# Inverse roots of the attention norms moved from GpSimd's power to ScalarE's logarithm and exponential, page scales made earlier, modulation rows started later

## The chip, the cores and the metric

The kernel runs on one core of a Trainium2 chip. The metric is the device time of one launch in microseconds (us). Beside the timed runs there is one execution recorded by the hardware profiler; its rows give, for every engine, what ran when. The engines are PE (matrix products, with its weight loads as PEld), DVE (vector work), ACT (scalar functions), POOL (GpSimd) and SP, which here issues every DMA.

## The reference, cut to what matters

One transformer layer on a sequence of 1024 rows with 1024 channels, in float32. Two attention groups of eight heads share an input projection: chunked attention over a band (CA, head width 64) and latent attention (MLA, with a low-rank q of 256 and kv of 128, and heads of 64 + 32). All of their norms are root-mean-square norms, and it is the inverse roots of these that the change concerns:

```python
def rmsnorm(x, g):
    xf = x.astype(jnp.float32)
    y = xf * lax.rsqrt(jnp.mean(xf * xf, axis=-1, keepdims=True) + EPS)
    return (y * g.astype(jnp.float32)).astype(x.dtype)
...
    mod = jnp.dot(jax.nn.silu(c), w_ada[l]) + b_ada[l]
    sh_a, sc_a, g_a, sh_m, sc_m, g_m = jnp.split(mod, N_MOD, axis=-1)
    h = modulate(rmsnorm(x, g_attn_norm[l]), sh_a, sc_a)
    proj = jnp.dot(h, w_in[l])
    q_lat, kv_lat, k_rope, ca_qkv = jnp.split(proj, split_pts, axis=-1)
    q = jnp.dot(rmsnorm(q_lat, g_q_latent[l]), w_q_up[l])      # 8 heads x 96
    kv = jnp.dot(rmsnorm(kv_lat, g_kv_latent[l]), w_kv_up[l])  # 8 heads x (64 + 64)
    k = concatenate([k_nope, k_rope of all heads])
    q, k = rmsnorm(q, g_mla_q[l]), rmsnorm(k, g_mla_k[l])      # then rope on the last 32
    ...
    cq, ck = rmsnorm(ca[:, :, 0], g_ca_q[l]), rmsnorm(ca[:, :, 1], g_ca_k[l])
    ...
    x = x + g_a * (concat(o_mla, o_ca) @ w_out)
    h = modulate(rmsnorm(x, g_mlp_norm[l]), sh_m, sc_m)
    x = x + g_m * ((silu(gate) * val) @ w_down)                # conv of width 3 before silu
```

## The kernel before

All products are float32 made of three products of split values: each operand is cut into a `hi` part and a residue `lo` (helpers `hi_of` and `lo_of`, lines 73 to 82; their rows in the profile all say L77 or L82, whichever engine they are given). Instructions are written in program order for a tile scheduler, which fixes each engine's order when the kernel is built: it lets an instruction go ahead of earlier ones by modelled times and priorities, and `tc.issue_after(x)` adds an order by hand. A tile from a pool with n buffers waits until the tile n back is no longer read. At run time every engine works through its own list in order, and so does SP, whose DMAs wait for their buffers.

*The start (to about 70 us).* SP loads constants, the eight x tiles, `c_rep`, the weights `adaw` of the first modulation (`load_ada`, line 207, sixteen tiles in five buffers), and the gains. `page_scales` (line 220) reduces gains and bias table to power-of-two scales, some 36 small DVE instructions, one of them fed by a product over `ones` and one by a POOL power. The loop at line 263 makes the x norms. Then the loop at line 362 runs over eight blocks d of 128 channels: two DVE reductions with `adaw` (L369) give shift and scale of the block, `mod_transpose` (line 341) turns x, applies them on ACT and splits the result into pages hT[d, h] (h = 0: `hi` on ACT and residue on POOL; h = 1: `hi` on POOL and residue on DVE), and PE starts the first q/k projection from each page.

*The attention (to 710 us).* The score and value blocks of 32 units (`Unit`: one head and half of the queries; first 16 of CA, then 16 of MLA) are laid out one after another; between the blocks `pace` takes steps from `fillers`, the generators that make what later units need: `f_v(0)`, `f_qk(1)`, `f_qk(2)`, `f_v(1)`, `f_qk(3)`, `f_m` (the latents), `f_up(0)` and `f_up(1)` (MLA's up-projections, `f_up_steps`, line 581) and `f_oca`. Beside them `f_ada` (line 483) makes twelve pieces of later modulation rows, each from eight loads `aw` of 128 KB and eight DVE products into `aacc` (L492 for the first, L494 for the others). Loads and sums share pool A of three buffers.

*The norms.* `qk_norm` (line 416), the loop in `f_m` (line 539) and that in `f_up_steps` (line 606) follow one scheme. ACT copies the projection out of PSUM and squares it, DVE sums per head (or ACT while squaring, for the latents), and POOL takes the inverse root by `rsqrt_mean`:

```python
    def rsqrt_mean(r, ss, n, cols=None):
        sc = ss if cols is None else ss[:, cols]
        pool.tensor_scalar(sc, sc, 1.0 / n, EPS, op0=MUL, op1=ADD)
        pool.tensor_tensor(r, ss, nhalf[:].to_broadcast(list(r.shape)), op=ALU.pow)
```

Then POOL (CA, latents, MLA's rope part of k) or DVE (MLA's q and the rest of k) multiplies by the root. In `f_up_steps` q and k of a tile have sums and roots of their own (`uss`/`ur` and `kss`/`kr`), and POOL adds the rope part's `ssr` to k's (L641). The `raw` copies come from four buffers (`rtile`), the squares from two (`qtile`).

*Value tiles.* `v_tile` (line 448) takes a tile from a rotating pool and lets POOL set its columns of ones and zeros: for CA from six buffers at each use, for MLA eight tiles. POOL also sets the rows of ones of the key pages `kts` and the row buffer `mz` (L694 to L696).

After 710 us follow the output projection, the second norm (`r2`, one column at a time, by `rsqrt_mean`) and the channel layer, in which PE is busy nearly all the time.

Of the kernel before, what the change touches and what calls it, by code (L numbers as in the profile page):

```python
# [23 lines left out]
P = 128  # L24
# [38 lines left out]
def layer_kernel(ctx, tc, I, out):  # L63
# [3 lines left out]
    def f32(ap):  # L67
        return ap.bitcast(F32)
# [12 lines left out]
    def lo_of(eng, o, i, hi):  # L81
        (pool if eng == "p" else dve).tensor_tensor(o, i, f32(hi), op=SUB)  # L82
# [40 lines left out]


# [72 lines left out]

    xs = []
# [142 lines left out]
    def mod_transpose(src, k, h, row, pspool, psum_tag, pb, hpool, tag, tmp, nbuf, heng, leng):  # L341

        pt = pspool.tile([P, 512], F32, name=f"ht_ps{row}_{k}_{h}", tag=psum_tag, bufs=pb)
        for j in range(4):
            pe.transpose(pt[:, j * P:(j + 1) * P], src(j), ident[:])
        pg = hpool.tile([P, 2, 512], F32R, name=f"hT{row}_{k}_{h}", tag=tag, bufs=nbuf)
        a, b = modT[:, row, k:k + 1], modT[:, row + 1, k:k + 1]
        v = tmp.tile([P, 512], F32, name=f"hv{row}_{k}_{h}", tag="hv", bufs=2)
        if heng == "a":
            act.activation(pg[:, 0], pt[:], AF.Identity, scale=a, bias=b)  # L350
        act.activation(v[:], pt[:], AF.Identity, scale=a, bias=b)
        if heng != "a":
            hi_of(heng, pg[:, 0], v[:])
        lo_of(leng, pg[:, 1], v[:], pg[:, 0])
        return pg

    hT = {}
# [58 lines left out]
    def qk_norm(src_psum, nm, qn, j0):  # L416
# [8 lines left out]
        rsqrt_mean(r[:], ss[:], HD)  # L425
# [22 lines left out]
    def v_tile(pl, name, tag, bufs):  # L448
        v = pl.tile([P, 4, 2, 3, 64], F16, name=name, tag=tag, bufs=bufs)
        pool.memset(v[:, :, 0, 1], 1.0)  # L450
        pool.memset(v[:, :, 1, 1], 0.0)
        return v
# [30 lines left out]
    def f_ada():  # L483
        for m in (2, 3, 4):
            for n in range(4):
                acc = atile(f"aacc{m}_{n}")
                c0 = m * D + n * 256
                for k in range(ND):
                    w = atile(f"aw{m}_{n}_{k}")
                    sp.dma_start(w[:], I["w_ada"][k * P:(k + 1) * P, c0:c0 + 256])  # L490
                    if k == 0:
                        dve.tensor_scalar(acc[:], w[:], cs[:, 0:1], None, op0=MUL)  # L492
                    else:
                        dve.scalar_tensor_tensor(acc[:], w[:], cs[:, k:k + 1], acc[:], op0=MUL, op1=ADD)  # L494
                    if k % 2 and k < ND - 1:
                        yield 0
# [39 lines left out]
    def f_m():  # L536
        w = load_w("wm_", I["w_m"], NM)
        lat = {}
        for t in range(NT):
# [12 lines left out]
            pool.tensor_scalar(ss[:, 0:1], ss[:, 0:1], 1.0 / QR, EPS, op0=MUL, op1=ADD)  # L552
            rsqrt_mean(r[:], ss[:], KVR, cols=slice(1, 2))
# [27 lines left out]
    def f_up_steps(gr):  # L581
        if gr == 0:
            right.__exit__(None, None, None)
            for i in "4v3":
                G["cm" + i] = tc.tile_pool(name="gp" + i, bufs=1, side="right", reuse_waits="tile")
                G[i] = G["cm" + i].__enter__()
        wq = []
# [18 lines left out]
        for t in range(NT):  # L606
            h, j = divmod(t, 4)
            sl = slice(j * P, (j + 1) * P)
            if t % 2 == 0:
                mq[gr, t // 2] = g3([P, 2, 4, QK], F32, f"qn{gr}_{t}")  # L610
                mk[gr, t // 2] = g3([P, 2, 4, QK], F32, f"kn{gr}_{t}")
                mv[gr, t // 2] = v_tile(G["v"], f"vt{gr}_{t}", "Gv", 8)
# [3 lines left out]
            raw = rtile(f"uqr{gr}_{t}")  # L616
            act.activation(raw[:, :384], pt[:, :384], AF.Copy)
            sq = qtile(f"usq{gr}_{t}")
            act.activation(sq[:, :384], raw[:, :384], AF.Square)
            ss = cst.tile([P, 4], F32, name=f"uss{gr}_{t}", tag="ss", bufs=4)  # L620
            r = cst.tile([P, 4], F32, name=f"ur{gr}_{t}", tag="rr", bufs=4)
            dve.tensor_reduce(ss[:], sq[:, :384].rearrange("p (a b) -> p a b", a=4), axis=AX.X, op=ADD)
            rsqrt_mean(r[:], ss[:], QK)
            q_t = mq[gr, t // 2][:, t % 2]
            dve.tensor_tensor(q_t, raw[:, :384].rearrange("p (a b) -> p a b", a=4),
                              r[:].unsqueeze(2).to_broadcast([P, 4, QK]), op=MUL)
            rope_apply(q_t[:, :, NOPE:], q_t[:, :, NOPE:], tabq, t, 4, raw[:, 0:256])
# [10 lines left out]
            ss = cst.tile([P, 4], F32, name=f"kss{gr}_{t}", tag="ss", bufs=4)  # L638
            r = cst.tile([P, 4], F32, name=f"kr{gr}_{t}", tag="rr", bufs=4)
            dve.tensor_reduce(ss[:], s3, axis=AX.X, op=ADD)  # L640
            pool.tensor_tensor(ss[:], ss[:], ssr[:, t:t + 1].to_broadcast([P, 4]), op=ADD)  # L641
            rsqrt_mean(r[:], ss[:], QK)
            k_t = mk[gr, t // 2][:, t % 2]
            dve.tensor_tensor(k_t[:, :, 0:NOPE], r3, r[:].unsqueeze(2).to_broadcast([P, 4, NOPE]), op=MUL)
            pool.tensor_tensor(k_t[:, :, NOPE:], kr[:, t:t + 1, :].to_broadcast([P, 4, ROPE]),
                               r[:].unsqueeze(2).to_broadcast([P, 4, ROPE]), op=MUL)
# [47 lines left out]
    for x in kts:  # L694
        pool.memset(x[64:65, 1], 1.0)
    pool.memset(mz[:], 0.0)  # L696
# [585 lines left out]
```

## Time and profile before

| | |
|---|---|
| timed runs | 1506.06, 1506.7, 1516.16 us; median 1506.7 |
| profiled execution | 1507.0 us, of which its span 1505.2 |
| mean granted PE clock | 0.945 |
| PE busy | 1323.0 us (88%), 6926 products |
| DVE busy | 1011.6 us (67%) |
| POOL busy | 818.5 us (54%) |
| ACT busy | 715.4 us (48%) |
| DMA | 153.02 MB, mean 102 GB/s |

Times are microseconds from the start of the span. An engine's busy time is a mean over stages of different kinds, so the prediction reads it stage by stage. In a group's row stand line, engine, operation, tiles out<-in with their sizes, the count, then busy time and mean ns, and behind the last bar the time in which the engine stood idle just before, with the instruction that ended most of it. In a row of the timeline the first number is the start and the second the length.

### The profile page before, as it was taken

The numbers are of one execution on the slowest core, as the hardware profiler recorded it, in microseconds if no ns is written. First come the engines' busy times: TensorE is split into PE (matmuls) and PEld (weight loads), VectorE is DVE, ScalarE is ACT, GpSimd is POOL, SyncE is SP. The second block draws the span as 40 slices with busy tenths as digits, with TensorE's granted clock in tenths as the row PEclk, the third lists the DMA queues.
The fourth block names the chain that finished last, engine by engine and source line by source line (L and its number), as shares of the span: only waits on it lengthen the run. The fifth ranks groups of instructions, "written<-read, shape, count | busy, mean of one in ns | idle before, by whom it ended". The sixth has DMA issues, their size and how long they took to land.

```text
span 1505.2 us, 19968 instructions
## 1 busy us (share of the span) xinstructions
PE 1323.0 (88%) x6926; PEld 1054.2 (70%) x6926; DVE 1011.6 (67%) x1421; ACT 715.4 (48%) x1319; POOL 818.5 (54%) x901
## 2 busy tenths in 40 slices
PE   3769999898868899988928759999999999999997
PEld 2769879776745556655716648888888887887885
DVE  8926665555667866565676668777777888666563
ACT  5435565454756766665453324444444433333331
POOL 5764444353698443322867245555556554665662
PEclk9979999999977999999958979999999999999999
DMA  8421223221110023324521142222222234446442
GB/s 308 124 67 50 64 61 111 80 74 43 57 35 8 18 82 98 103 81 149 211 98 56 56 154 84 85 84 84 78 77 84 85 123 172 147 145 231 163 140 98
DMA packets 80001, 153.02 MB, mean 102 GB/s; under 512 B 8214, under 2 KB 44314, under 8 KB 79900
## 3 DMA queue, kind: packets, MB, share of 16 engines
q1 hardware_dynamic: 79900, 151.75, 30.5%
q8 instruction: 54, 0.88, 0.3%
q14 instruction: 47, 0.39, 0.1%
HBM read 122.88 MB, written 28.84 MB: 101 GB/s over the span
## 4 chain that ended last, share of the span: by engine, by line
PE 34%; DVE 18%; POOL 16%; DMA 16%; issue 10%; ACT 5%; DVEq 0%; SPq 0%; POOLq 0%; ACTq 0%
DMA aw<-w_ada 7%; POOL wds L82 4%; DMA wu<-w_up 4%; PE tm L815 3%; DVE u L1132 3%; PE dnp L1196 2%; PE dnp L1197 2%; PE dnp L1198 2%; PE p L1126 2%; PE p L1124 2%; PE p L1125 2%; DVE aacc L494 2%; DVE wu L1154 2%; DVE u L1133 2%; DVE adaw L369 1%
## 5 line engine op out<-in xcount | busy, mean ns | idle before, releaser
L82 POOL TENSOR_TENSOR wds<-wd,wds 128x512 fp32r<-128x512 f32 x88 | 152.9, 1756 | 100.2 <-ACT wds L75 100.2
L75 ACT ACTIVATE wds<-wd 128x512 fp32r<-128x512 f32 x88 | 54.6, 624 | 152.2 <-PE dnp L1198 149.6
L1196 PE MATMUL dnp<-wds,g 128*128 128x512 f32 x308 | 119.7, 390 | 2.3 <-DVE c L1158 1.5
L1186 DVE TENSOR_TENSOR wd<-wd,gmbc 128x1024 f32<-128x1024 f32 x44 | 69.9, 1588 | 76.3 <-DMA wd<-w_down 76.2
L1198 PE MATMUL dnp<-wds,g 128*128 128x512 f32 x308 | 118.5, 390 | 2.2 <-DVE g L82 2.2
L1197 PE MATMUL dnp<-wds,g 128*128 128x512 f32 x308 | 119.7, 389 | 0.0
L82 POOL TENSOR_TENSOR wc<-ws,wc 128x512 fp32r<-128x512 f32 x22 | 55.4, 2520 | 74.2 <-ACT wc L75 74.2
L494 DVE SCALAR_TENSOR_TENSOR aacc<-aw,cs,aacc 128x256 f32<-128x256 f32 x84 | 45.4, 541 | 62.5 <-DMA aw<-w_ada 62.1
L82 POOL TENSOR_TENSOR wa<-wu,wa 128x512 fp32r<-128x512 f32 x22 | 36.7, 1669 | 90.6 <-ACT wa L75 90.6
L815 PE MATMUL tm<-qt,kt 96*128 96x512 f16 (+7 forms) x288 | 74.1, 346 | 7.7 <-ACT qt L778 4.7
L826 DVE TENSOR_TENSOR hlm<-pm,hlm 128x512 f16<-128x512 f32 (+1 forms) x96 | 58.3, 615 | 32.6 <-POOL hlm L77 17.8
L1132 DVE SCALAR_TENSOR_TENSOR u<-c,pk,u 128x1023 f32<-128x1023 f32 x44 | 75.5, 1724 | 4.1 <-ACT u L1131 4.1
L82 DVE TENSOR_TENSOR g<-gr,g 128x512 fp32r<-128x512 f32 x44 | 70.6, 1607 | 9.9 <-ACT g L75 9.9
L819 ACT ACTIVATE pc<-tc,sca 128x512 f32<-128x512 f32 (+3 forms) x96 | 50.2, 524 | 47.5 <-DVE hlc L826 27.9
L815 PEld LDWEIGHTS <-kt 128*128 128x128 f16 (+2 forms) x480 | 47.4, 102 | 35.2 <-issue 16.8
L77 POOL TENSOR_SCALAR hlm<-pm 128x384 f16<-128x384 f32 (+2 forms) x48 | 24.8, 516 | 82.9 <-ACT pm L819 65.1
L1196 PEld LDWEIGHTS dnp<-wds,g 128*128 128x128 f32 x308 | 57.8, 188 | 15.6 <-ACT wds L75 1.9
L1198 PEld LDWEIGHTS dnp<-wds,g 128*128 128x128 f32 x308 | 57.8, 188 | 15.0 <-DVE g L82 3.0
L819 ACT ACTIVATE pm<-tm,scm 128x512 f32<-128x512 f32 (+1 forms) x96 | 55.3, 579 | 27.2 <-PE tm L815 20.6
L1131 ACT ACTIVATE u<-c,pk 128x1024 f32<-128x1024 f32 x44 | 52.3, 1236 | 32.9 <-DVE c L1164 32.9
L826 DVE TENSOR_TENSOR hlc<-pc,hlc 128x512 f16<-128x512 f32 (+3 forms) x96 | 52.8, 553 | 22.5 <-POOL hlc L77 11.9
L1197 PEld LDWEIGHTS dnp<-wds,g 128*128 128x128 f32 x308 | 57.8, 188 | 11.9
(432 smaller groups left out, 4703.1 us busy)
## 6 DMA issues: line engine op xcount, KB each, us to landing
wu<-w_up SPq DMA_DIRECT2D x44, 512.0 KB, 3.5
wd<-w_down SPq DMA_DIRECT2D x44, 512.0 KB, 3.6
aw<-w_ada SPq DMA_DIRECT2D x96, 128.0 KB, 2.1
g_d<-u SPq DMA_DIRECT2D x22, 512.0 KB, 2.6
gr<-g_d SPq DMA_DIRECT2D x44, 256.0 KB, 2.8
x<-x SPq DMA_DIRECT2D x16, 512.0 KB, 7.1
adaw<-w_ada_a SPq DMA_DIRECT2D x16, 512.0 KB, 5.1
wq_r<-w_qk SPq DMA_DIRECT2D x32, 128.0 KB, 2.4
```

Of the source, the lines that this page charges most:

```text
L75: act.activation(o, i, AF.Copy)
L82: (pool if eng == "p" else dve).tensor_tensor(o, i, f32(hi), op=SUB)
L494: dve.scalar_tensor_tensor(acc[:], w[:], cs[:, k:k + 1], acc[:], op0=MUL, op1=ADD)
L815: last = pe.matmul(s[:, c0:c1], l, m, start=(y == 0), stop=(y == len(todo) - 1))
L819: act.activation(p[:, :w], s[:, :w], AF.Exp, scale=ninv)
L826: dve.tensor_tensor(hl[:, 1, :w], p[:, :w], hl[:, 0, :w], op=SUB)
L1131: act.activation(u[:], c, AF.Identity, scale=pk[:, cv + 2:cv + 3], bias=pk[:, cv + 3:cv + 4])
L1132: dve.scalar_tensor_tensor(u[:, 1:], c[:, :S - 1], pk[:, cv + 1:cv + 2], u[:, 1:], op0=MUL, op1=ADD)
L1186: dve.tensor_tensor(raw[:], raw[:], gmbc[:], op=MUL)
L1196: pe.matmul(pts[t][n], sh, w[n][:, 0], start=(j == 0), stop=False)
L1197: pe.matmul(pts[t][n], sh, w[n][:, 1], start=False, stop=False)
L1198: pe.matmul(pts[t][n], sl, w[n][:, 0], start=False, stop=(j == NF - 1))
```

## The change

A new helper `rsqrt_att` takes the place of `rsqrt_mean` in the three attention norms: DVE scales the mean and adds epsilon, ACT takes the logarithm and the exponential of minus half of it, and three DVE instructions make one Newton step. In `f_up_steps` q's and k's sums lie in one tile of eight columns and get one root together, after k's projection; the order of the code below it follows, and `ssr` is added on DVE. `page_scales` and the load of the gains are written ahead of `load_ada(0)` and the x loads. The value tiles are made once for each stage, and set on DVE, as are the rows of `kts` and `mz`. Each piece's first product in `f_ada` is held behind the last DVE residue of the first pages (`last_lo["v"]`). The x norms, the second norm and `pow2_scale` keep their POOL power.

```diff
     def lo_of(eng, o, i, hi):
-        (pool if eng == "p" else dve).tensor_tensor(o, i, f32(hi), op=SUB)
+        return (pool if eng == "p" else dve).tensor_tensor(o, i, f32(hi), op=SUB)
...
+    def rsqrt_att(rr, ss, nm, ns):
+        w = ss.shape[-1]
+        if len(ns) == 1:
+            dve.tensor_scalar(ss, ss, 1.0 / ns[0], EPS, op0=MUL, op1=ADD)
+        else:
+            for i, n in enumerate(ns):
+                dve.tensor_scalar(ss[:, i:i + 1], ss[:, i:i + 1], 1.0 / n, EPS, op0=MUL, op1=ADD)
+        t = cst.tile([P, 8], F32, name=f"rt{nm}", tag="rt", bufs=4)[:, :w]
+        act.activation(t, ss, AF.Ln)
+        act.activation(rr, t, AF.Exp, scale=-0.5)
+        dve.tensor_tensor(t, rr, rr, op=MUL)
+        dve.scalar_tensor_tensor(t, t, -0.5, ss, op0=MUL, op1=MUL)
+        dve.scalar_tensor_tensor(rr, t, 1.5, rr, op0=ADD, op1=MUL)
...
+    gn = st.tile([P, 4 * HD + 17], F32, name="gn")
+    sp.dma_start(gn[:], I["gains"])
     xs = []
...
-    load_ada(0)
 
     def page_scales():
-        gn = st.tile([P, 4 * HD + 17], F32, name="gn")
-        sp.dma_start(gn[:], I["gains"])
...
     page_scales()
+    load_ada(0)
...
-        lo_of(leng, pg[:, 1], v[:], pg[:, 0])
+        last_lo[leng] = lo_of(leng, pg[:, 1], v[:], pg[:, 0])
...
-        rsqrt_mean(r[:], ss[:], HD)
+        rsqrt_att(r[:], ss[:], nm, (HD,))
...
-    def v_tile(pl, name, tag, bufs):
-        v = pl.tile([P, 4, 2, 3, 64], F16, name=name, tag=tag, bufs=bufs)
-        pool.memset(v[:, :, 0, 1], 1.0)
-        pool.memset(v[:, :, 1, 1], 0.0)
-        return v
+    def v_tiles(pl, name, n):
+        vs = [pl.tile([P, 4, 2, 3, 64], F16, name=f"{name}{i}") for i in range(n)]
+        for v in vs:
+            dve.memset(v[:, :, 0, 1], 1.0)
+            dve.memset(v[:, :, 1, 1], 0.0)
+        return vs
+
+    vca = v_tiles(at, "vca", 6)
...
-                    vts[2 * pp + i, h] = v_tile(at, f"v{2 * pp + i}_{h}", "v16", 6)
+                    vts[2 * pp + i, h] = vca[(4 * pp + 2 * i + h) % 6]
...
                     if k == 0:
-                        dve.tensor_scalar(acc[:], w[:], cs[:, 0:1], None, op0=MUL)
+                        with tc.issue_after(last_lo["v"].ins):
+                            dve.tensor_scalar(acc[:], w[:], cs[:, 0:1], None, op0=MUL)
...
-            pool.tensor_scalar(ss[:, 0:1], ss[:, 0:1], 1.0 / QR, EPS, op0=MUL, op1=ADD)
-            rsqrt_mean(r[:], ss[:], KVR, cols=slice(1, 2))
+            rsqrt_att(r[:], ss[:], f"m{t}", (QR, KVR))
...
+            G["vs"] = v_tiles(G["v"], "vm", 8)
...
-            raw = rtile(f"uqr{gr}_{t}")
+            uq = rtile(f"uqr{gr}_{t}")
...
-            ss = cst.tile([P, 4], F32, name=f"uss{gr}_{t}", tag="ss", bufs=4)
-            r = cst.tile([P, 4], F32, name=f"ur{gr}_{t}", tag="rr", bufs=4)
-            dve.tensor_reduce(ss[:], ..., axis=AX.X, op=ADD)
-            rsqrt_mean(r[:], ss[:], QK)
-            q_t = mq[gr, t // 2][:, t % 2]
-            dve.tensor_tensor(q_t, ...)          # and rope_apply on q_t
+            ss = cst.tile([P, 8], F32, name=f"uss{gr}_{t}", tag="ss", bufs=4)
+            r = cst.tile([P, 8], F32, name=f"ur{gr}_{t}", tag="rr", bufs=4)
+            dve.tensor_reduce(ss[:, 0:4], ..., axis=AX.X, op=ADD)
...
-            dve.tensor_reduce(ss[:], s3, axis=AX.X, op=ADD)
-            pool.tensor_tensor(ss[:], ss[:], ssr[:, t:t + 1].to_broadcast([P, 4]), op=ADD)
-            rsqrt_mean(r[:], ss[:], QK)
+            dve.tensor_reduce(ss[:, 4:8], s3, axis=AX.X, op=ADD)
+            dve.tensor_scalar(ss[:, 4:8], ss[:, 4:8], ssr[:, t:t + 1], None, op0=ADD)
+            rsqrt_att(r[:], ss[:], f"u{gr}_{t}", (QK,))
+            q_t = mq[gr, t // 2][:, t % 2]
+            dve.tensor_tensor(q_t, ...)          # and rope_apply on q_t
...
     for x in kts:
-        pool.memset(x[64:65, 1], 1.0)
-    pool.memset(mz[:], 0.0)
+        dve.memset(x[64:65, 1], 1.0)
+    dve.memset(mz[:], 0.0)
```

More of the change, by code (lines that the diff above doesn't have):

```diff
@@ L637, in f_up_steps @@
             act.activation(s3, r3, AF.Square)
[L638 to L641, printed above, removed]
-            rsqrt_mean(r[:], ss[:], QK)
+            dve.tensor_reduce(ss[:, 4:8], s3, axis=AX.X, op=ADD)
+            dve.tensor_scalar(ss[:, 4:8], ss[:, 4:8], ssr[:, t:t + 1], None, op0=ADD)
+            rsqrt_att(r[:], ss[:], f"u{gr}_{t}", (QK,))
+            q_t = mq[gr, t // 2][:, t % 2]
+            dve.tensor_tensor(q_t, uq[:, :384].rearrange("p (a b) -> p a b", a=4),
+                              r[:, 0:4].unsqueeze(2).to_broadcast([P, 4, QK]), op=MUL)
+            rope_apply(q_t[:, :, NOPE:], q_t[:, :, NOPE:], tabq, t, 4, uq[:, 0:256])
             k_t = mk[gr, t // 2][:, t % 2]
-            dve.tensor_tensor(k_t[:, :, 0:NOPE], r3, r[:].unsqueeze(2).to_broadcast([P, 4, NOPE]), op=MUL)
+            dve.tensor_tensor(k_t[:, :, 0:NOPE], r3, r[:, 4:8].unsqueeze(2).to_broadcast([P, 4, NOPE]), op=MUL)
             pool.tensor_tensor(k_t[:, :, NOPE:], kr[:, t:t + 1, :].to_broadcast([P, 4, ROPE]),
-                               r[:].unsqueeze(2).to_broadcast([P, 4, ROPE]), op=MUL)
+                               r[:, 4:8].unsqueeze(2).to_broadcast([P, 4, ROPE]), op=MUL)
     def f_up(gr):
```

12 lines of the change are left out of this document (5 added, 7 removed).

## The prediction

> **What bounds the kernel now.** I read the page's first lines, then the busy times by stage, then the chain that ended last inside each stage, then its waits.
>
> ```profile
> span 1505.2 us, 19968 instructions
> PE 1323.0 (88%) x6926; PEld 1054.2 (70%) x6926; DVE 1011.6 (67%) x1421; ACT 715.4 (48%) x1319; POOL 818.5 (54%) x901
> ```
> ```profile
> core 0: us, PE busy (x) PEld busy (x) DVE busy (x) ACT busy (x) POOL busy (x), PEclk, DMA share, GB/s
> 0.00:20.00 20.00, 3.60 (x8) 1.46 (x8) 14.78 (x59) 12.21 (x21) 11.69 (x24) 1.00 0.89 334
> 20.00:70.00 50.00, 38.38 (x246) 34.56 (x246) 49.38 (x102) 22.28 (x37) 31.76 (x31) 0.93 0.59 189
> 70.00:92.00 22.00, 7.36 (x33) 5.24 (x32) 7.41 (x13) 10.66 (x33) 20.95 (x41) 0.63 0.17 54
> 92.00:405.00 313.00, 289.05 (x2114) 252.70 (x2115) 183.52 (x387) 173.88 (x401) 142.00 (x261) 0.97 0.24 68
> 405.00:545.00 140.00, 114.95 (x560) 73.92 (x559) 103.25 (x236) 89.03 (x189) 103.80 (x195) 0.84 0.10 29
> 545.00:710.00 165.00, 148.91 (x830) 98.11 (x829) 96.55 (x181) 110.35 (x200) 49.38 (x59) 0.98 0.30 98
> ```
>
> The average (PE 88%) hides four regimes. From 20 to 70 us, where the first pages hT are made, DVE is busy 49.38 of 50. From 70 to 92 PE nearly stops and POOL is busy 20.95 of 22. From 92 to 405 and from 545 to 710 PE is busy over 90%. From 405 to 545, the MLA up-projections, PE falls to 82% at a granted clock of 0.84, and DVE and POOL are at 74% each. After 710 nothing that sets the time is edited. The chain agrees: DVE, then the POOL power, then the last load of w_v:
>
> ```profile
> 49.37 2.17 DVE adaw L369
> 82.48 1.64 POOL r L120
> 87.77 2.36 DMA wv_r<-w_v
> ```
>
> **The change part by part.** Four stages, each with its own sum.
>
> *Stage 1, 20 to 70 us: DVE loses work.* The first modulation row (eight products) leaves for the time after the last DVE page residue, and `page_scales` moves ahead of the x scaling. What both cost on DVE here:
>
> ```profile
> L494 DVE SCALAR_TENSOR_TENSOR aacc<-aw,cs,aacc 128x256 f32<-128x256 f32 x7 | 3.8, 537 | 0.0
> L230 DVE SCALAR_TENSOR_TENSOR gw<-pk 128x32 f32<-128x32 f32 x2 | 1.8, 923 | 0.0
> L230 DVE SCALAR_TENSOR_TENSOR gw<-gn 128x64 f32<-128x64 f32 (+1 forms) x3 | 1.7, 564 | 0.0
> L492 DVE TENSOR_SCALAR aacc<-aw,cs 128x256 f32<-128x256 f32 x1 | 1.4, 1366 | 0.0
> L246 DVE TENSOR_SCALAR gt<-gt 128x3 f32<-128x3 f32 x1 | 1.2, 1237 | 0.0
> L259 DVE TENSOR_TENSOR gk_ca<-gk_ca,sca 128x1 f32<-128x1 f32 x1 | 0.1, 145 | 0.0
> ```
>
> ```profile
> 43.48 1.27 POOL L82 TENSOR_TENSOR hT<-hv,hT 128x512 fp32r<-128x512 f32 x1 [1.63 <-ACT hv L351]
> 43.52 1.24 DVE L232 TENSOR_TENSOR gt<-gt 128x1 f32<-128x1 f32 x1
> ```
>
> Row products: 3.8 + 1.4 = 5.2 us. Page scales: 1.8 + 1.7 (L230), 1.2 (L246), 1.2 (L232, which ends only when the POOL instruction above it is done), and 29 more at about 0.145 (L259) = 4.2. Together 15.3 us, about 13.5 since short ones overlap at their ends. The page scales now run before 20 us, where DVE has 20 - 14.8 = 5.2 us free; but their load goes ahead of the x loads on SP, and their one POOL power ahead of three x norms. I charge 1 us. DVE alone would give 12.5. PE gives less:
>
> ```profile
> 24.50:71.60 47.10, 39.78 (x258) 36.16 (x259) 46.08 (x94) 22.11 (x37) 31.09 (x31) 0.93 0.53 161
> 69.60 0.69 DVE L82 TENSOR_TENSOR hT<-hv,hT 128x512 fp32r<-128x512 f32 x1 [0.52 <-POOL hT L77]
> 28.22 0.41 PE L156 MATMUL qk_s<-wq_s,hT 128*128 128x256 f32 x1
> 28.43 0.41 PE L154 MATMUL qk_s<-wq_s,hT 128*128 128x256 f32 x1
> 71.37 0.28 PE L154 MATMUL qk<-wq_s,hT 128*128 128x256 f32 x1
> 71.49 0.28 PE L155 MATMUL qk<-wq_s,hT 128*128 128x256 f32 x1
> ```
>
> Its idle time between the first product (24.5) and the last (71.6) is 47.1 - 39.8 = 7.3 us, so that much comes at once. More needs the shorter start distance of 71.37 to 71.49 (0.12 us) in place of that of 28.22 to 28.43 (0.21); a PE fed without holes should hold it more often. Bounds 5 and 13; I take 9.5, nearer PE's figure. The last DVE residue then ends at about 61 instead of 70.3.
>
> *Stage 2, the gap from 70 to 92: one chain replaced by another.*
>
> ```profile
> L120 POOL TENSOR_TENSOR r<-ss,nhalf 128x8 f32<-128x8 f32 x4 | 6.5, 1650 | 0.1
> L695 POOL MEMSET kt<- 1x512 f16 x4 | 2.2, 574 | 0.1
> L450 POOL MEMSET v<- 128x256 f16 x6 | 1.8, 305 | 0.0
> ```
>
> POOL loses the four powers (6.5) and the memsets (2.2, 1.8 and as much for the zero halves). But the added order on DVE puts the row's first product behind the last residue; behind that stand 17 memsets and then the first reduction, and the row's other products, each behind its own load, stand between the reductions for which ACT and POOL wait. Prices that this trace has for the new pieces:
>
> ```profile
> L768 DVE MEMSET sc<- x32: 112/112/112, 123.2 to 409.4; 64x64 f32 x32
> L411 DVE SCALAR_TENSOR_TENSOR hb<-hb,hb 128x8 f32<-128x8 f32 x1 | 0.2, 156 | 0.0
> 3.13 0.21 ACT L105 ACTIVATE cs<-pk 128x8 f32<-128x8 f32 x1 [1.13 <-DMA pk<-pack]
> ```
>
> Memsets: 17 x 0.112 = 1.9 us at least, 12 x 0.305 + 4 x 0.574 + 0.2 = 6.2 at POOL's rows; I take 4.5, since the sizes are those of POOL's. One inverse root is four DVE instructions of 0.156 and two on ACT of 0.21: 1.05 us, but six handovers. Following SP's queue: the bias load waits for the bias buffer (some 6 us after the last residue), the row's loads wait for its products one by one, and the last two w_v loads stand behind all of these and POOL's residues. I get the last w_v load on the chip about 18.5 us after the last residue; before it was 90.1 (87.77 + 2.36) - 70.3 = 19.8. So this stage gives 1.3, not POOL's 12. Bounds: 8 (POOL's time comes out in full down to the loads) and -4 (memsets at POOL's price and each load exposed).
>
> *Stage 3, 92 to 405: POOL is relieved where it did not bind.*
>
> ```profile
> DVE aacc L494 <- DMA aw<-w_ada: 61.5, 48, 3.4
> POOL ss L119 <- DVE ss L424: 27.0, 11, 4.8
> PE sc L755 <- DVE mz L771: 10.1, 9, 2.4
> ```
>
> Here 12 norms of q and k and 8 of the latents change sides. POOL saves 12 x 1.65 (L120's row of stage 2) and 8 x about one, some 28 us, of which PE sees little: POOL is busy 142 of 313. DVE takes 12 x 4 + 8 x 5 = 88 more instructions of 0.156 = 14 us, on a queue that already stands 61.5 us behind modulation loads and on which PE waits (10.1 us). The 27 us that POOL stood waiting for the sums of squares become waits of ACT's logarithm, and what is queued behind that on ACT is the exponentials that PE's value products need. I charge 3 us; bounds 10 (a quarter of those 27 and 14 us) and -6 (POOL's hi pages come earlier by its wait and power).
>
> *Stage 4, 405 to 545: the only stage where POOL's powers sit on the chain.*
>
> ```profile
> L120 POOL TENSOR_TENSOR kr<-kss,nhalf 128x4 f32<-128x4 f32 x16 | 16.6, 1035 | 0.7
> L120 POOL TENSOR_TENSOR ur<-uss,nhalf 128x4 f32<-128x4 f32 x16 | 16.4, 1025 | 0.4
> L119 POOL TENSOR_SCALAR uss<-uss 128x4 f32<-128x4 f32 x16 | 5.2, 328 | 5.0 <-DVE uss L622 3.1 <-DVE vsm L402 0.9
> L641 POOL TENSOR_TENSOR kss<-kss,ssr 128x4 f32<-128x4 f32 x16 | 4.4, 275 | 4.3 <-DVE kss L640 4.3
> L119 POOL TENSOR_SCALAR kss<-kss 128x4 f32<-128x4 f32 x16 | 3.5, 222 | 1.3
> ```
>
> 16.6 + 16.4 + 5.2 + 4.4 + 3.5 = 46 us leave POOL (103.8 to 58). DVE gets 16 x 5 x 0.156 = 12.5 and 16 memsets, some 4: 103.3 to 120 of 140, and is next to bind. Were DVE as full as in stage 1 (99%), the stage would take 121; at 91% 132. q now waits for k's half too, so its page comes later by one product and two squares, which the four raw buffers cover for two tiles. I take 8; bounds 14 and -3.
>
> Row L232 above took 1.24 us for one element per partition, until POOL was done, against 0.145 for the same form in L259; so a small DVE instruction can stand behind POOL without a semaphore. [...] By the row alone, one such case in L259's dozen neighbours, I stay at 8.
>
> *Everything after 545*: no instruction that PE waits for is changed; 0, ±2.
>
> Sum against the profiled execution's own time, 1507.0 (span 1505.2 and 1.8 around it; the median of the runs shown is 1506.7): 1507.0 - 9.5 - 1.3 + 3 - 8 = 1491.2, told as 1491.
>
> **The rivals.**
> (a) DVE binds stage 4, which gives nothing. For it: 120 of 140 us and the in-order handovers DVE to ACT and back; against it: POOL and DVE are equally busy there now, and POOL loses 46 us where DVE gains 16. 1491 + 8 = 1499.
> (b) POOL's relief reaches PE everywhere: stage 1 at 12, stage 2 at 3, stage 3 at -2 (earlier hi pages), stage 4 at 13. For it: PE's clock, 0.63 in stage 2 and 0.84 in stage 4, could rise with its load; against it: stage 3's PE is 92% full. 1507 - 12 - 3 - 2 - 13 = 1477.
> (c) Stage 1 was not DVE's alone: the row's products only move into the gap, the modulation loads or PE set the pace, and the two stages give 2 where I say 11. For it: PE busy 39.8 of 47.1; against it: the chain there names DVE alone. 1491 + 9 = 1500.
> (d) Slower: ACT stands on its logarithm until DVE, itself behind a modulation load, has the sum of squares, and the exponentials behind it come late. Its place is stage 3 and the start of stage 4. The 27.0 us of POOL's waits plus 4.3 + 3.1 in stage 4 (L641, L119) reach PE in full, and stage 4 gives nothing: 1507 - 10.8 + 34.4 = 1531; half of it 1513. The time is above the old one once 10.8 us, a third of these waits, reach PE. Against it: ACT arrives later than POOL did, and PE holds two score blocks ahead.
>
> **How the numbers follow.** Forecast 1491 (own range 1483 to 1499) 0.45; (a) 0.17; (b) 0.18; (c) 0.08; (d) 0.12. One per cent, about what a measurement of this kernel tells from no change, is 15 us: 1491.6 to 1521.8 is "the same". Faster: 0.26 of the forecast and all of (b), 0.44. Slower: the upper part of (d), 0.09. Same: the rest, 0.47. The bounds add to 1507 - 13 - 8 - 6 - 14 - 2 = 1464 and 1507 - 5 + 4 + 10 + 3 + 2 = 1521; the range leaves out their corners: 1472 to 1514.
>
> **What would show it right or wrong.** Right: the last DVE residue of hT near 61 us, the first dense value products near 82; no row of L120 on POOL between 70 and 545 but single columns; POOL under 70 us and DVE over 115 in the up-projection stage, which lasts some 132. Wrong: DVE idle in stage 1 while PE runs without holes (c); new waits "ACT rt <- DVE ss" of over 15 us in all and PE under 90% after the gap (d); the up-projection stage still 140 us long with DVE over 90% (a).

## The result and the profile after

The changed kernel takes 1499.8 us (median of 11 runs, 1496.37 to 1506.18); the kernel before, on the same chips, 1512.7 (11 runs, 1506.06 to 1516.16). The ratio is 0.9924, 95% interval 0.9904 to 0.9944: some 11.5 us faster, about three quarters of one per cent. The prediction said 1491 from 1507, a ratio of 0.9894. The time lies in its range of 1472 to 1514, but 0.8 us above the 1483 to 1499 that the forecast had for itself, and next to the 1499 and 1500 of rivals (a) and (c). Part of that distance is the start: the sum began at the profiled execution's 1507.0, and the median of the kernel before is 1512.7. By the prediction's one per cent the result is "the same", to which it gave 0.47; the interval leaves no doubt that the kernel is faster. The parts of the sum did not come as told.

The page and the busy times by stage of the changed kernel (columns as before: stretch, its length, busy time and count of PE, PEld, DVE, ACT, POOL, granted clock, DMA share, GB/s):

```profile
span 1497.0 us, 20054 instructions
PE 1317.5 (88%) x6926; PEld 1053.8 (70%) x6926; DVE 1048.2 (70%) x1638; ACT 725.6 (48%) x1399; POOL 730.9 (49%) x728
```
```profile
20.00:70.00 50.00, 35.56 (x242) 32.71 (x243) 44.45 (x76) 22.69 (x37) 34.63 (x32) 0.93 0.55 174
70.00:92.00 22.00, 9.38 (x45) 7.26 (x44) 19.48 (x52) 13.13 (x43) 10.42 (x16) 0.67 0.32 97
92.00:405.00 313.00, 293.50 (x2116) 256.69 (x2115) 200.54 (x497) 178.75 (x443) 102.63 (x192) 0.96 0.23 68
405.00:545.00 140.00, 112.07 (x595) 73.06 (x594) 115.82 (x315) 98.12 (x226) 64.02 (x117) 0.91 0.12 35
```

From 20 to 70 us DVE has 26 instructions fewer but only 5 us less busy time, and PE does less than before, not more. In the gap DVE (19.48 of 22) has taken POOL's place. In the up-projections POOL fell from 103.8 to 64.0 and DVE rose from 103.3 to 115.8 (58 and 120 were worked out).

Both kernels were profiled a second time (the runs before_again and after_again below), so each step can be read as a difference of means. The times are first starts and last ends in the views of single tiles; the 24th product of the first value projection (ipv, called v product here) is counted in PE's timeline.

| us from the span's start | before, twice | after, twice | step, measured | step, predicted |
|---|---|---|---|---|
| last residue of hT ends | 70.3, 70.5 | 68.9, 68.3 | -1.8 | -9.5 |
| 24th v product ends | 93.3, 93.5 | 92.0, 91.7 | +0.2 | -1.3 |
| first q up-projection (qu) | 405.1, 407.9 | 400.2, 403.8 | -3.0 | +3 |
| last k up-projection ends (ku) | 530.0, 532.7 | 521.8, 526.2 | -2.8 | -8 |
| first output projection (op) | 704.1, 707.1 | 692.6, 697.5 | -3.2 | 0 |
| end of the span | 1505.2, 1509.3 | 1497.0, 1500.3 | +2.0 | 0 |

The sum is -8.6 us; the medians, which lie 4 us further apart, are the better figure for the whole. The front gave 1.6 where 10.8 was forecast, the middle gave 3 where it was to cost 3, and the up-projections with what follows them gave 6.

The front is best read in DVE's groups from 20 us to the last residue. Before:

```profile
L369 DVE CUSTOM_DVE_ANT_0 adaw<-adaw,csb,pk 128x1024 f32<-128x1024 f32 x8 | 12.7, 1586 | 0.0
L369 DVE CUSTOM_DVE_ANT_0 adaw<-adaw,csb,bsc 128x1024 f32<-128x1024 f32 x8 | 10.4, 1306 | 0.0
L370 DVE TENSOR_TENSOR modT<-adat,pk 128x1 f32<-128x1 f32 x8 | 5.2, 648 | 0.0
```

After:

```profile
L384 DVE CUSTOM_DVE_ANT_0 adaw<-adaw,csb,pk 128x1024 f32<-128x1024 f32 x8 | 14.2, 1775 | 0.0
L384 DVE CUSTOM_DVE_ANT_0 adaw<-adaw,csb,bsc 128x1024 f32<-128x1024 f32 x8 | 12.1, 1514 | 0.0
L385 DVE TENSOR_TENSOR modT<-adat,pk 128x1 f32<-128x1 f32 x8 | 7.0, 874 | 0.0
```

The same instructions on the same data became longer by 5.0 us in all. What they wait for stands in the timelines of DVE and POOL; here one round of the changed kernel, and PE beside it:

```profile
54.73 1.72 DVE L384 CUSTOM_DVE_ANT_0 adaw<-adaw,csb,pk 128x1024 f32<-128x1024 f32 x1
56.38 1.75 DVE L384 CUSTOM_DVE_ANT_0 adaw<-adaw,csb,bsc 128x1024 f32<-128x1024 f32 x1
58.17 1.18 DVE L385 TENSOR_TENSOR modT<-adat,pk 128x1 f32<-128x1 f32 x1
59.27 1.82 DVE L384 CUSTOM_DVE_ANT_0 adaw<-adaw,csb,pk 128x1024 f32<-128x1024 f32 x1
61.11 0.68 DVE L82 TENSOR_TENSOR hT<-hv,hT 128x512 fp32r<-128x512 f32 x1
```
```profile
55.34 1.70 POOL L82 TENSOR_TENSOR wv_s<-wv_r,wv_s 128x256 fp32r<-128x256 f32 x1
58.07 1.27 POOL L82 TENSOR_TENSOR hT<-hv,hT 128x512 fp32r<-128x512 f32 x1 [1.03 <-ACT hv L365]
59.30 0.72 POOL L82 TENSOR_TENSOR wv_s<-wv_r,wv_s 128x256 fp32r<-128x256 f32 x1
```
```profile
58.01 0.28 PE L170 MATMUL ipv<-wv_s,hT 128*128 128x256 f32 x1
61.84 0.58 PE L170 MATMUL qk<-wq_s,hT 128*128 128x256 f32 x1 [3.55 <-DVE hT L82]
```

They take turns. POOL's residue of w_v starts at 55.34 and takes 1.70, against 0.72 for the next one, because the adaw product holds until 56.45; the adaw product started at 56.38 takes 1.75, against 1.27 undisturbed, because POOL holds until 57.04; one column of modT takes 1.18 and ends with POOL's instruction (59.35 and 59.34). In this round DVE is never idle, and PE waits 3.55 us for a residue behind all this.

Behind the last adaw product (it ends at 64.5 before and 61.1 after) the picture is another. The tail up to the last residue, before and after, and pieces of the chain through it after:

```profile
64.50:70.30 5.80, 4.81 (x41) 4.61 (x40) 5.28 (x24) 2.23 (x3) 3.09 (x6) 1.00 0.16 45
```
```profile
61.10:68.90 7.80, 7.06 (x40) 7.06 (x41) 2.28 (x8) 2.90 (x4) 3.10 (x8) 0.62 0.01 2
```
```profile
61.84 0.58 PE qk L170
63.92 0.87 PE ht_ps L359 x4
65.49 0.78 ACT hv L365
66.34 1.29 POOL hT L82
67.62 0.60 POOL hT L77
68.24 0.69 DVE hT L82
```

After, PE works without a hole from the end of its wait (61.84) on, at a granted clock of 0.62 where it was 1.00, and DVE stands idle for 5.5 us before its last two residues: it waits for POOL, POOL for ACT, and ACT for the products with which PE turns x (ht_ps). In this tail PE sets the pace.

### The profile page after: what moved, and what is told of

Same layout as the page of the kernel before. It is cut to its first block, busy times and chain, and to the rows that moved or that the text cites. A ratio compares the mean times of both kernels' runs of the same rounds, so it can differ in the third digit from the quotient of the medians.

```text
span 1497.0 us, 20054 instructions
## 1 busy us (share of the span) xinstructions
PE 1317.5 (88%) x6926; PEld 1053.8 (70%) x6926; DVE 1048.2 (70%) x1638; ACT 725.6 (48%) x1399; POOL 730.9 (49%) x728
## 4 chain that ended last, share of the span: by engine, by line
PE 62%; DVE 16%; DMA 11%; ACT 4%; POOL 3%; issue 3%; SPq 0%; DVEq 0%; ACTq 0%; POOLq 0%
PE p L1142 9%; PE p L1140 9%; PE p L1141 9%; DMA aw<-w_ada 7%; PE dnp L1214 4%; PE dnp L1213 4%; PE dnp L1212 4%; PE tm L831 3%; DVE aacc L513 2%; DVE adaw L384 2%; DVE mz L787 1%; PE op L170 1%; PE op L168 1%; PE op L169 1%; DVE hlc L842 1%
## 5 line engine op out<-in xcount | busy, mean ns | idle before, releaser
L842 DVE TENSOR_TENSOR hlm<-pm,hlm 128x512 f16<-128x512 f32 (+1 forms) x96 | 55.1, 580 | 34.8 <-POOL hlm L77 17.6
L77 POOL TENSOR_SCALAR hlm<-pm 128x384 f16<-128x384 f32 (+2 forms) x48 | 24.3, 506 | 93.3 <-ACT pm L835 73.2
L1149 DVE SCALAR_TENSOR_TENSOR u<-c,pk,u 128x1022 f32<-128x1022 f32 x44 | 63.7, 1483 | 0.0
L835 ACT ACTIVATE pm<-tm,scm 128x512 f32<-128x512 f32 (+1 forms) x96 | 55.2, 579 | 17.0 <-PE tm L831 11.5
```

The lines of the kernel that those rows point to most:

```text
L835: act.activation(p[:, :w], s[:, :w], AF.Exp, scale=ninv)
L842: dve.tensor_tensor(hl[:, 1, :w], p[:, :w], hl[:, 0, :w], op=SUB)
```

## The experiments

Ratios are to the kernel before on the same chip, with 95% intervals.

### The front part alone (e1_front)

The kernel before with these edits of the change only:

```diff
+    gn = st.tile(...); sp.dma_start(gn[:], I["gains"])     # ahead of the x loads
+    page_scales(); load_ada(0)                             # in this order
+                        with tc.issue_after(last_lo["v"].ins):   # first product of each piece
```

> The kernel before with the front part of the change alone: page scales ahead of the x loads, the first product of each modulation piece held behind the last DVE residue. Roots and memsets as before. Theory P (port): in the first 70 us DVE's instructions with two inputs and POOL's shut each other out; what was taken off DVE was for the most part waiting for POOL, and the wait goes over to the next instruction. The last residue of hT ends at 67.5 to 70 us (70.3 before), the mean of the 16 adaw products rises from 1.45 to 1.6 us or more, the time falls by 1 (between -4 and +2). Rival D (the prediction's): DVE's 13.5 us come out up to PE's bound; the last residue ends near 61, adaw stays at 1.45, the time falls by 9.5, and what ate it in the full change are the memsets and roots at 70 us.

Measured: last residue 69.6, first latent product at 305.9 exactly as before, mean of the adaw products 1.645 us (1.446 before). Up to 400 us the front part gives nothing, as theory P had it. The time is 0.9975 (0.9963 to 0.9988) of before; these 3.8 us come after 405 us, where no instruction was edited (see e10_double).

The page scales show what the removed rows were made of. In this part of the change they are only moved, and the changed kernel has them in the first 20 us, where POOL works on single columns of the x norms:

```profile
L243 DVE SCALAR_TENSOR_TENSOR gw<-gn 128x64 f32<-128x64 f32 (+1 forms) x3 | 0.6, 200 | 0.0
L243 DVE SCALAR_TENSOR_TENSOR gw<-pk 128x32 f32<-128x32 f32 x2 | 0.4, 193 | 0.0
L259 DVE TENSOR_SCALAR gt<-gt 128x3 f32<-128x3 f32 x1 | 0.2, 160 | 0.0
```

These are L230 and L246 of the prediction's rows: 1.7 + 1.8 + 1.2 = 4.7 us there, 1.2 us here. Three quarters of their time was waiting for POOL.

### Residues from POOL to the full DVE (e5_vv)

The changed kernel, the h = 0 residue of each page on DVE:

```diff
-                                     hw, "hT", st, 16, "ap"[h], "pv"[h])
+                                     hw, "hT", st, 16, "ap"[h], "vv"[h])
```

> The changed kernel, with the eight residues of the first pages that POOL made (h = 0, 1.59 us each) on DVE (0.68 us where undisturbed). Theory P (port): DVE's two-input instructions and POOL's take turns, so the turn of 1.24 us is replaced by one of 0.68; the last residue ends 4 us earlier (65 for 68.9), the mean of the 16 adaw products falls from 1.64 to 1.45 us or less, the time falls by 3 (+1 to -6). Rival D (DVE is the bound by its own work): DVE, never idle from 20 to 61 us, gets 5.4 us more; the last residue ends at 73 to 75, the time rises by 4.

DVE's groups in the same stretch:

```profile
L82 DVE TENSOR_TENSOR hT<-hv,hT 128x512 fp32r<-128x512 f32 x16 | 13.7, 856 | 1.3 <-POOL hT L77 0.7 <-ACT hv L365 0.6
L384 DVE CUSTOM_DVE_ANT_0 adaw<-adaw,csb,bsc 128x1024 f32<-128x1024 f32 x8 | 11.5, 1442 | 0.0
L384 DVE CUSTOM_DVE_ANT_0 adaw<-adaw,csb,pk 128x1024 f32<-128x1024 f32 x8 | 11.0, 1374 | 0.0
L385 DVE TENSOR_TENSOR modT<-adat,pk 128x1 f32<-128x1 f32 x8 | 2.8, 346 | 0.0
```

DVE, "99% busy", was given eight instructions more and ended 6.7 us earlier (last residue 62.2 for 68.9): modT fell from 7.0 to 2.8, adaw from 26.3 to 22.5. Theory P holds with a larger gain than said (4), D is out. Of the 6.7 us, 3.7 are won up to the last adaw product (it ends at 57.4 in place of 61.1) and 3.0 behind it, where PE has no hole and its granted clock is 1.00. The dense v products follow (86.9 for 92.0), and the lead stands at 6.4 us at the first latent product. From the last k up-projection (518.3 for 521.8) to the first output projection it goes again (696.1 for 692.6), and the time is 0.9934 (0.9913 to 0.9955), no gain on the changed kernel. Why it goes there is open: in that stretch PE is busy 156.5 us at a granted clock of 0.95, against 153.0 at 0.98 in the changed kernel, and idle 21.3 us against 17.8.

### The roots alone (e2_roots), in CA alone (e3_qk), in the up-projections alone (e4_up)

The kernel before with `rsqrt_att` and only these calls; first all three of

```diff
-        rsqrt_mean(r[:], ss[:], HD)
+        rsqrt_att(r[:], ss[:], nm, (HD,))             # qk_norm: also e3_qk
-            rsqrt_mean(r[:], ss[:], KVR, cols=slice(1, 2))
+            rsqrt_att(r[:], ss[:], f"m{t}", (QR, KVR))  # latents
+            rsqrt_att(r[:], ss[:], f"u{gr}_{t}", (QK,)) # merged up-projection root: also e4_up
```

> The kernel before with the new roots in all three places alone (up-projections merged); memsets on POOL, front as before. Theory R: POOL's relief is what gives the time from 100 to 700 us. The first product of the latents (mp) comes 5 us earlier (300.9 for 305.9), the first output projection 9 us earlier (695 for 704.1), the time falls by 9 (-6 to -12). Rival F: the gain of the middle stage came from the front (modulation pieces later, memsets off POOL); then mp first stays within 2 us of 305.9 and the time falls by 4 or less. The prediction's stage 3 would have it 3 us later.

> The kernel before with the new root in qk_norm alone (16 calls); latents and up-projections keep POOL's power. Theory R: mp first 4 us earlier (302), nothing more after 310 us, time -4 (-1 to -7). Rival F: mp first within 2 us of 305.9, time within 2 us. The prediction's stage 3 (ACT stands on its logarithm): mp first 2 to 3 us later.

> The kernel before with the new, merged root in the up-projections alone. Up to 400 us nothing changes (qu first within 1 us of 405.1). The prediction's stage 4: the last k projection comes 8 us earlier (522 for 530.0), time -8. Theory M (seen in the changed kernel's trace: 3.5 us lost in the first two tiles, then 1.5 us per tile pair won, and won further between 530 and 700): last k projection 3 us earlier (527), first output projection 6.5 us earlier (697.5), time -6.5 (-3 to -9). Rival A (DVE binds): both within 2 us, time within 2 us.

| | ratio to before | first score product (tc) | first latent product | last ku ends | first op |
|---|---|---|---|---|---|
| before (first profile) | 1 | 101.1 | 305.9 | 530.0 | 704.1 |
| roots alone | 0.9918 (0.9891 to 0.9946) | 88.1 | 296.6 | 520.3 | 695.7 |
| CA alone | 0.9964 (0.9945 to 0.9983) | 88.0 | 299.9 | 523.9 | 702.0 |
| up-projections alone | 0.9939 (0.9919 to 0.9959) | 101.3 | 306.4 | 523.7 | 698.0 |
| whole change | 0.9924 (0.9904 to 0.9944) | 95.1 | 298.2 | 521.8 | 692.6 |

The roots alone have the whole gain. Theory R holds for the middle stage, with nearly twice the size (9.3 us at the first latent product). All profiles of this document agree: from the 24th v product to the first latent product the five without CA's new root (before twice, e1_front, e4_up, e10_double) take 209.5 to 212.7 us, the nine with it 204.8 to 209.2.

The up-projections' root alone gives 6.1 us by the first output projection: theory M's size, won earlier than M said (6.3 by the last ku, where the prediction had 8). But the length of its own stage does not tie this to the root. From the first qu to the end of the last ku, the kernels that keep POOL's power there take 124.9 and 124.8 us (before), 121.4 (e1_front), 123.2 (e10_double) and 119.7 (e3_qk), though none of these has an edit in that stage; those with the new root take 116.0 to 124.9, among them 117.0 in e4_up and 124.8, 124.7 and 124.9 in e5_vv, e11_pmem and e18_rvh.

Part of the middle's gain is that the gap is filled: with roots alone the first scores are made at 88 in place of 101, while PE still waits for w_v. From 72 to 92 us, before, CA alone, and the changed kernel:

```profile
72.00:92.00 20.00, 5.47 (x17) 3.55 (x17) 6.28 (x10) 9.16 (x31) 19.03 (x36) 0.59 0.19 60
```
```profile
72.00:92.00 20.00, 10.06 (x42) 7.92 (x43) 11.84 (x33) 11.67 (x41) 15.73 (x33) 0.57 0.27 83
```
```profile
72.00:92.00 20.00, 7.38 (x28) 5.29 (x27) 17.63 (x42) 11.90 (x41) 10.42 (x16) 0.63 0.33 100
```

PE makes 42 products in place of 17 there with CA's roots, and 28 in the whole change, whose memsets and modulation row fill DVE (17.63 of 20).

### The power twice (e10_double)

The kernel before:

```diff
         rsqrt_mean(r[:], ss[:], HD)
+        pool.tensor_tensor(r[:], ss[:], nhalf[:].to_broadcast([P, 8]), op=ALU.pow)   # qk_norm
```

> The kernel before with POOL's power in qk_norm run twice (16 more of 1.65 us on POOL, the result is the same); no wait for a DVE sum is added. Taking power and scaling away from there gave 9.3 us by 212 us and 6.0 by mp first. Theory Q (the time POOL's queue is held counts): the reverse, 2.5 us later at the first 24 v products, mp first 6 us later (312 for 305.9), time +5 (+2 to +10). Rival W (what counted was POOL's wait for DVE's sums, 27.0 us): mp first within 2 us, time within 2.

From the 24th v product to the first latent product, before and with the power twice:

```profile
93.30:305.90 212.60, 200.31 (x1562) 180.68 (x1561) 126.19 (x270) 113.95 (x245) 89.85 (x134) 0.99 0.25 73
```
```profile
93.80:303.30 209.50, 199.81 (x1566) 180.87 (x1565) 125.56 (x271) 114.86 (x248) 110.76 (x149) 0.99 0.26 75
```

POOL has 21 us more to do and the stretch is 3 us shorter. In the dense stretch the length of POOL's powers sets nothing; theory Q holds only in the gap (first score 105.2 for 101.1). Rival W is not shown either: it said no change within 2 us, and the waits were not taken away alone. And the kernel is faster than before: 0.9967 (0.9949 to 0.9986). Adding work that changes no result made it 5 us faster, as e1_front's untouched stages made it 4 us faster. Such a kernel's order on all engines is laid out anew at every build, so an effect under some 5 us is not tied to its edit by the time alone.

### Memsets back on POOL (e11_pmem) and modulation loads held (e14_hold)

The changed kernel with `dve.memset` of `v_tiles`, `kts` and `mz` as `pool.memset`; and, on its own:

```diff
+                    with tc.issue_after(last_ld["wv0_"].ins):        # SP: the last w_v load
                         sp.dma_start(w[:], I["w_ada"][...])          # aw of f_ada
```

> The changed kernel with all memsets back on POOL. The prediction had 4.5 us of memsets on DVE's path in the gap from 70 to 92 us. Theory G (gap bound by loads): the first score product comes 5 us earlier (90 for 95.1), but the w_v loads stand where they were, so the first 24 v products end within 1.5 us of 92.0 and the time stays within 4 us. Rival M (memsets bind): they end 4 us earlier, 88, and so does all that follows up to 300 us (mp first 294 for 298.2), time -4.

> The changed kernel with the loads aw of the modulation rows, too, held behind the last w_v load on SP. In the changed kernel six of them stand ahead of the last two w_v loads and wait for buffers that DVE's products free. Theory G (the gap ends with the last w_v load on the chip): the last one lands near 82 instead of 88.3, the first 24 v products end at 86 to 88 (92.0), mp first 4 us earlier (294), time -4 (-1 to -8). Rival: bias loads or POOL's residues hold w_v up as much; then the first 24 v products end within 1.5 us of 92.0 and the time stays within 3.

With the memsets on POOL the first score comes at 89.8, yet the 24th v product ends at 93.2 and the first latent product is at 298.7 (92.0 and 298.2): theory G up to 300 us, M is out. The whole is worse than forecast, 0.9982 (0.9967 to 0.9998), and the loss comes after the first latent product: against the mean of the changed kernel's two profiles it is 2.0 us behind at the first qu, 4.7 at the end of the last ku (528.7) and 7.8 at the end. The sixteen memsets of MLA's value tiles run on POOL in one piece ahead of this (379 to 384 us); that this is the cause was not tried apart.

With the loads held the order on SP is, in the chain of the changed kernel first and then in SP's timeline with the loads held:

```profile
86.03 2.32 DMA wv_r<-w_v
```
```profile
73.41 1.58 SPq L204 DMA_DIRECT2D wv_r<-w_v  x3
79.69 1.46 SPq L204 DMA_DIRECT2D wv_r<-w_v  x2
81.59 0.33 SPq L511 DMA_DIRECT2D aw<-w_ada  x1
```

The last two w_v loads leave at 79.69 to 81.15 in place of 86.03, and the 24th v product ends at 89.0, 3.0 us earlier; 3.2 us stand at the first latent product. So the gap ends with a load queued behind others, though sending it earlier gained less than told (86 to 88 for the 24th v product). Another wait took its place: DVE's L409, the 128x8 product for v's scale, took 2.67 us through four POOL residues in a row (84.90 to 87.69), where the same row took 0.45 in the changed kernel, and PE waited 1.04 us for it. The time is 0.9929 (0.9904 to 0.9954), the same as the changed kernel's, where 4 us less were expected: as in e5_vv the lead, 6.5 us at the end of the last ku, is gone at the first output projection (694.1 for 692.6).

### Once more, and two versions with both edits (before_again, after_again, e17_vvhold, e18_rvh)

> The kernel before, unchanged, profiled a second time. Its first profiled execution (1507.0) lies 5 us under its median of 1512.5. If the 5 us are the granted clock's (theory C), the second execution has the same times within 0.5 us up to 400 us (first 24 v products 93.3, mp first 305.9), and differs in stages where PE has holes, by half of the difference in the time at half clock, most of it after 400 us. If the order of handovers differs from run to run (rival), times differ before 400 us already.

> The changed kernel, unchanged, profiled a second time. Theory C: last residue 68.9, first 24 v products 92.0, mp first 298.2 again, each within 0.5 us; up-projections (400 to 522 in the first execution) and the rest differ by half of the difference in the time at half clock (20.5 us in the up-projections in the first execution). Rival: times before 300 us differ by over 1 us.

> The changed kernel with all residues of the first pages on DVE and the modulation loads held behind the last w_v load, the two edits that moved the dense v products from 92.0 to 86.9 and 89.0. If both act on the same end (last w_v load): first 24 v products at 84 to 87, mp first at 289 to 292, time 6 us under the changed kernel's (1494; ratio to before 0.988). Rival L (what is won before 500 us goes again between 610 and 700 us, as e5_vv showed: 10 us): time within 3 us of the changed kernel's.

> The kernel before with the new roots, page scales ahead, all residues of the first pages on DVE, modulation loads held behind the last w_v load; memsets stay on POOL at each use, and DVE's products of the first row have no order by hand. If memsets on DVE have no value of their own: first 24 v products at 84 to 87, time as e17's within 3 us. If the 4 us that the kernel with all memsets on POOL lost against the roots alone came from making the value tiles ahead, this one is the faster by 3 to 5.

The second profiles (1511.1 and 1502.1 us) are those of the table above. Up to the first latent product the kernel before repeats within 0.7 us, the changed one only within 1.7. Theory C asked for 0.5 and is not borne out, and the rival's sign (over 1 us before 300) shows in the changed kernel; at the first qu the two executions differ by 2.8 and 3.6 us.

The changed kernel with all residues of the first pages on DVE and the modulation loads held (e17_vvhold) takes 1497.5, ratio 0.9891 (0.9874 to 0.9909). By the ratios that is 5 us under the changed kernel, about as expected, though its first latent product stands at 295.2 in place of 289 to 292. The kernel before with the roots, the page scales and these two edits, but memsets left on POOL (e18_rvh), takes 1496.3, ratio 0.9883 (0.9863 to 0.9903); the 24th v product ends at 84.5 as expected. Both beat the kernel before, and by their ratios the changed kernel's 0.9924 (0.9904 to 0.9944), whose interval they just meet or just miss. Between the two no difference shows, so the memsets on DVE have no value that can be seen here (e18_rvh also leaves out the order by hand of the modulation products, so this is said of both together).

## Why the prediction was right, and where its steps were wrong

*Stage 1 (-9.5 said, -1.8 measured).* The step that failed is "Row products ... Page scales ... together 15.3 us": the durations of the rows taken off were counted as DVE's work. Of the 13.5 us that stayed after the allowance for overlap, 4.8 came out. Most of the rest was waiting for POOL, and it went over to the instructions that stayed (5.0 us of it to adaw and modT). From the first adaw product to the end of the last one, the stretch shrank from 44.7 to 39.9 us, 4.8, the removed work proper; 1.4 of this went since that first product starts later (21.2 for 19.8; 1 was charged), and 2.0 in the tail, which grew from 5.8 to 7.8: PE, after its wait of 3.55 us, worked there at a granted clock of 0.62 (0.77 and 7.5 us in the second profile). The 9.5 that PE was to allow were never reached, but in the tail PE set the pace, and there the sign of rival (c), DVE idle while PE runs without holes, did show, for 5.5 us; in the rounds before it DVE stayed full. Rival (c) had the price (2 of 11), for the most part for another reason.

The row that could have told it was quoted: L232, 1.24 us for one element. It was read as one case in a dozen, while L230, L246 and L492 in the same fence (923, 1237 and 1366 ns for some 200, 160 and 350) were others. That a small DVE instruction can stand behind POOL was weighed for stage 4 alone; the trace shows it in stage 1, where modT went from 874 to 346 ns when POOL's residues of hT were given to DVE. What makes the two engines take turns, for which theory P names a port, no run shows, nor whether two inputs on DVE are a condition: L246, with one input, was long as well (1.24 us from 60.32 on, 0.16 in the changed kernel) and ended at 61.56, with the POOL residue that ended at 61.53.

*Stage 2 (-1.3 said, +0.2 measured).* The step itself was sound: a last w_v load behind the modulation row on SP. It lands 19.4 us after the last residue (18.5 said, 19.8 before), and holding the row's loads moves it. What was left out is that PE can work inside the gap. The "near 82" for the first dense value products (92.0) was missed mostly by stage 1's error.

*Stage 3 (+3 said, -3.0 measured, -5.0 by the first latent product).* The failed step is "I charge 3 us". The waits came as described. They stand in the waits of the changed kernel from 92 to 405 us:

```profile
DVE aacc L513 <- DMA aw<-w_ada: 53.9, 56, 2.8
POOL qn L441 <- DVE r L137: 17.9, 9, 5.6
ACT rt L133 <- DVE ss L128: 9.7, 7, 2.7
ACT rtm L133 <- DVE mss L131: 8.7, 4, 4.2
```

POOL's 27.0 us became 18.4 on ACT and 17.9 on POOL, so rival (d) had its waits, above the 15 us that were to show it. PE shows no loss by them: it was idle 12.3 us between the 24th v product and the first latent product before (212.60 - 200.31) and 8.5 after:

```profile
92.00:298.20 206.20, 197.66 (x1550) 179.65 (x1549) 131.07 (x312) 114.54 (x264) 65.11 (x105) 0.99 0.25 74
```

That is 3.8 of the 6.4 us of the first pair of profiles (2.3 of 3.5 in the second); twelve products fewer, some of them made in the gap, are the rest. What closed the holes is open: not the length of the power.

*Stage 4 (-8 said, -2.8 there and -6.0 with what follows).* The signs held: POOL 64.0 (under 70 said), DVE 115.8 (over 115 said). The five instructions added for each root on DVE cost more than was worked out (12.5 said):

```profile
L653 DVE TENSOR_SCALAR uss<-uss,ssr 128x4 f32<-128x4 f32 x16 | 4.6, 289 | 0.1
L136 DVE SCALAR_TENSOR_TENSOR rtu<-rtu,uss 128x8 f32<-128x8 f32 x16 | 3.4, 216 | 0.2
L135 DVE TENSOR_TENSOR rtu<-ur 128x8 f32<-128x8 f32 x16 | 3.3, 207 | 1.1 <-ACT ur L134 1.0
L137 DVE SCALAR_TENSOR_TENSOR ur<-rtu,ur 128x8 f32<-128x8 f32 x16 | 2.9, 179 | 0.2
L128 DVE TENSOR_SCALAR uss<-uss 128x8 f32<-128x8 f32 x16 | 2.8, 173 | 0.2
```

These are 17.0 us. As an edit of its own the root brought the last ku 6.3 us earlier and 9 in time, which is nearly the size. But the term of 8 is a claim on the length of this stage, and that length moves by as much between kernels that do not differ there (119.7 to 124.9 with POOL's power, 116.0 to 124.9 with the new root). So the runs do not show what the root is worth in its stage, and why 2.8 came in place of 8 stays open. In the whole change less of it shows in the stage: the second 12 q products end 11.7 us after the first there (405.1 to 416.8; 8.2 before), then it gains. That the merged root is late for the first tiles, as "q now waits for k's half" had it, fits; it was not tried apart. The end of the stage is also blurred by the clock, in the up-projections before and after:

```profile
405.10:530.00 124.90, 103.17 (x511) 67.29 (x509) 93.07 (x218) 80.89 (x172) 94.28 (x183) 0.85 0.09 23
```
```profile
400.20:521.80 121.60, 97.65 (x534) 65.63 (x532) 104.36 (x299) 85.97 (x205) 55.07 (x108) 0.92 0.09 24
```

The granted share is 0.07 higher, over 122 us some 8.5 us of full clock, yet PE's idle time grew by 2.2 us (21.7 to 23.9). The two profiles of the changed kernel show how this goes: at 0.87 in place of 0.92 PE's busy time in this stage is 101.9 us in place of 97.7, its idle time 20.5 in place of 23.9, and the stage is only 0.8 us longer. Here a slower clock filled PE's holes first. What sets the clock was not shown; in the changed kernel it was 0.67 in the gap, where PE was busy 9.38 of 22 us, and 0.96 in the stage after it, where PE was busy 293.50 of 313.

*After 545 us (0 ± 2 said).* -3.2 by the output projection and +2.0 behind it. The stretch up to the output projection takes 170.8 to 178.8 us in the profiles of this document, so the 3.2 are not tied to an edit either. The 2.0 lie between the last output projection and the first product of the down projection (498.1 and 497.8 us before; 500.7 and 499.7 after), which is nowhere edited; the other profiles all have 499.7 to 501.9, and it is open.

The total was near because a front that was overrated by 9 and up-projections overrated by 5 there were set against a middle and an end underrated by 6 and 3. That these errors met was luck. What the prediction had right is that the roots are worth moving; it looked for their gain in the up-projections, and the runs show it in the middle stage.

## What to carry to other kernels

A duration in a profile can hold waiting. Here DVE and POOL took turns in the first 70 us, and the waiting is inside the busy row (one column of modT: 1.18 us beside a POOL residue, 0.15 undisturbed): compare the same form where the other engine is quiet before you count what a removal gives. When an engine is full for that reason, moving an instruction to the engine that does it in the shorter turn can help even if that engine is the full one (here residues of 0.68 us on DVE for such of 1.27 on POOL: the last one ended 6.7 us earlier, with no gain in the whole time). And before an effect of a few microseconds is put down to an edit, look whether an edit that should do nothing moves the time as far.

## What the runs showed of the hardware that was not expected

One column of 128 elements on DVE took 1.24 us beside a POOL residue and 0.15 alone, and the eight of the stage 7.0 us. In the changed kernel's 44.45 busy us of DVE from 20 to 70 us, about 14 were waiting (an estimate from the undisturbed durations): adaw 26.3 less 16 x 1.27, modT 7.0 less 8 x 0.15, and the residues' 7.6 less 8 x 0.68. Two profiled executions of one program differed by 4.1 and 3.3 us in their spans: the kernel before by 3.5 us between the first latent product and the first qu alone (99.2 and 102.7), the changed one by 2.0 already between the 24th v product and the first latent product (206.2 and 208.2), where PE is 96% busy. After a hole of 3.55 us PE worked for some 7 us at a granted clock of 0.62 in one execution; in the other the clock of this tail was 0.77.
